# Neighbourhood attention in a two-layer hybrid block: value products of two heads side by side on the column halves of the array

## The chip, the core and the metric

The kernel runs on one core of one Trainium2 chip. The metric is device time in microseconds (us); lower is better. The engines of the core are named as in the profile: PE (TensorE, the matrix multiplier; PEld is its weight load), DVE (VectorE), ACT (ScalarE), POOL (GpSimd), and SP, whose queue issues most transfers. A matmul reads its stationary operand (the weights) and its moving operand from on-chip memory and writes PSUM; DVE and ACT copy PSUM back.

## The reference, cut to what matters

The block has two layers over 512 latent tokens (a grid of 8 rows by 64 columns) and 256 context tokens, with 1024 features. Layer 0 mixes tokens with eight neighbourhood-attention heads of 64 features and four mLSTM heads, layer 1 with latent attention; each layer ends with a gated feed-forward network. All of it is computed to float32 accuracy. The part at issue is the neighbourhood attention:

```python
s_lat = jnp.einsum('bqhd,bkhd->bhqk', q_row, k_band).astype(jnp.float32) * scale + bias
s_ctx = jnp.einsum('bqhd,bkhd->bhqk', q_row, k_c).astype(jnp.float32) * scale
p = jax.nn.softmax(jnp.concatenate([s_lat, s_ctx], axis=-1), axis=-1).astype(v.dtype)
return (jnp.einsum('bhqk,bkhd->bqhd', p[..., :nl], v_band)
        + jnp.einsum('bhqk,bkhd->bqhd', p[..., nl:], v_c))
```

The context tokens have an attention of their own over the 256 context keys (`dense_attention`), with the same heads.

## The kernel before

**How the work is tiled.** The queries of a head are cut into four column strips of the grid, 128 queries each (index `j`). A strip sees 256 latent keys (two key tiles of 128) and the 256 context keys (two more), so its scores are one PSUM tile of 128 queries by 512 keys, named `sp`. Softmax runs along that row: DVE adds the bias and takes the maximum, ACT takes the exponential, POOL divides by the sum; the result is `P[j]`.

**Value products.** For the product with the values, keys must lie on the partitions. For a key tile `ks` the kernel transposes the four `P[j]` on PE into a PSUM tile `ptp`, copies it to `pT` (128 keys by 512 queries), and multiplies: `vtok` (128 keys by 64 features of one head) is the stationary operand, `pT` the moving one. The output `ops` has the 64 features on its partitions: head 0 of a pair on partitions 0 to 63, head 1 on 64 to 127 (`rows`). So each product uses 64 of the array's 128 columns, which the profile shows as the form `128*64` (rows by columns of the array in use). Key tiles 2 and 3 (context) are one product of 512 columns; key tiles 0 and 1 (latent) are four of 128 columns, since each strip has its own values. These operands are plain float32, and the trace has two matmul records for each such instruction. The context tokens go the same way: `scores_c`, the transposes `ptc`, the copy `pTc`, and two products of 256 columns into `opc`.

**Order.** Pairs of heads run one after the other (`p_` 0 to 3). While a pair is in attention, `fill(n)` puts in steps of the projections of the next pair (`qp`, `kp`, `vp`, and the transposes `vtp` that make the next `vtok` from the copies `vt`); while the last pair is in attention, steps of the output projection (`yps`). The scores and projections use another float32 format (one record each). A scheduler places each engine's instructions once, before the run; on the chip each engine goes through its list in that order. In `before` a head is taken alone: `weighted(0)`, then `weighted(1)`, then `weighted_c` for either head.

**Other names.** `whi` and `wlo` are the two parts of a weight unit of 1024 columns, split by ACT and DVE from the loaded `wraw`; `spc`, `mxc`, `lsc` and `Pc` are scores, maximum, sum and weights of the context tokens; `mix` takes the outputs of all heads; `av` and `aw` belong to the modulation of layer 1, which DVE works out during the last pair; `fcw` holds the convolution weights of the feed-forward networks.

Of the kernel before, what the change touches and what calls it, by code (L numbers as in the profile page):

```python
# [9 lines left out]
F32 = mybir.dt.float32  # L10
# [8 lines left out]
TX = 512  # L19
TC = 256  # L20
T = TX + TC
# [45 lines left out]
def hybrid_backbone_kernel(ctx: ExitStack, tc: tile.TileContext, *aps):  # L67
# [14 lines left out]
    def psum_open(**n):  # L82
        """n: tiles per tag; A tiles hold two banks, the others one"""
        if psum:
            psum["st"].close()
        st = ExitStack()
        psum["st"], psum["n"], psum["split"] = st, n, False
        psum["p"] = st.enter_context(tc.tile_pool(name="ps" + "".join(f"{k}{v}" for k, v in n.items()), bufs=1,
                                                  space=bass.MemoryType.PSUM, reuse_waits="tile"))
# [41 lines left out]
    fcw = cload("ffn_conv", [128, 2, 2 * NH, 4])  # L131
# [26 lines left out]
    def table(func, after):  # L158
        """has the activation table loaded ahead of its first use"""
# [23 lines left out]
    def proj(o, w, x, cols, ks=tuple(range(KD)), first=True, last=True):  # L183
        """out[m, cols] = sum over k tiles of W[k, m]^T x[k, cols]; w units hold [k][128]."""
# [60 lines left out]
    def ada(l, part, get, pool, bufs):  # L245
        """modulation part (1024 columns) of layer l; column group j of the array takes 256 of them"""
# [19 lines left out]
    def ada_q(l, part, q, get, pool, bufs):  # L266
        """256 columns of a part; column group j of the array takes a quarter of the k tiles"""
# [16 lines left out]
    def ada_v(l, part, hf, nv, get, pool):  # L284
        """half a part of the modulation on the vector engine: the k tiles are scaled and added up, then the
        tensor engine sums over the partitions"""
# [40 lines left out]
    def mod_scale(l, part, norm, name, nv=2):  # L327
        """norm_g * (1 + scale)"""
# [14 lines left out]
    class Seg:  # L343
        """a run of tokens: width, offset in the padded layout, offset in the packed one, modulation column"""
# [12 lines left out]
    def rstd_bc(pss, n, dim, name):  # L357
        """PSUM [128, n*128]: rstd of every token on all partitions"""
# [16 lines left out]
    def step(n):  # L375
        """n steps of the norm chains in flight, oldest first"""
# [7 lines left out]
    def until(sg):  # L384
        """finish the chain of a run of tokens"""
# [3 lines left out]
    def sums4(ps, w, srcs, first, last):  # L389
        """column sums of four tiles, side by side in the array"""  # L390
# [4 lines left out]
    def sums_bc(ps, sg, name):  # L395
        """rstd on all partitions from the sums of sums4"""
# [7 lines left out]
    class YNorm:  # L404
        """sum of squares over the feature tiles of a branch output, then the gated residual"""
# [27 lines left out]
        def chain(self, x, y, Gt, mod=None, done=None):  # L433
            """x(k) += y(k) * rstd * G, then h hi/lo = split(x(k) * rstd * A + B) with mod = (A, B, h), or done(k);
            a feature tile per step, y as scratch"""
# [38 lines left out]
    # =============================== layer 0 ===============================  # L474
# [4 lines left out]
    with ExitStack() as l0:  # L479
# [38 lines left out]
        def x0_scale(q):  # L518
            """x * rstd * A for a quarter of the feature tiles"""
# [16 lines left out]
        def token_major(which, wus):  # L536
            """W[k, 512] with tokens on the output partitions; a k tile per step"""
# [39 lines left out]
        # gate rows, four feature tiles side by side in the array; the shift comes in with the bias  # L577
# [58 lines left out]
        # tri[:, 0]: k <= m ; tri[:, 1]: k >= m ; tri[:, 2]: row 127 ; tri[:, 3]: row 0  # L636
# [12 lines left out]
        # additive masks: msk[:, 0] allows column <= row, msk[:, 1] allows column >= row  # L649
# [9 lines left out]
        # running maxima of e along the scan, chunks and heads on partitions (the directions 32 apart)  # L659
# [52 lines left out]
        # -M in three exact pieces (rows 0, 32, 64 on), for its sums over the partitions to be rows of it  # L712
# [30 lines left out]
        def na_proj(p_, nq, res):  # L743
            """queries, keys and values of a pair of heads, in steps"""
# [46 lines left out]
        def na_attn(p_, nw, bias_t, fill, qs, kd, kl, vtok):  # L791
# [34 lines left out]
            def weighted(s, P):  # L826
                r0, r1 = rows[s]
                for ks in (2, 3, 0, 1):
# [4 lines left out]
                    pT = nw.tile([128, 512], F32, tag="pT", name="pT", bufs=2)  # L833
                    if ks % 2:
# [3 lines left out]
                    if ks >= 2:  # L838
                        mm(ops_[r0:r1, 0:TX], vtok[:, 7 + ks - 2, r0:r1], pT, ks == 2, False)
                    else:  # L840
                        for j in range(4):
                            vi = VTILE[KSTART[j] + 16 * ks]
                            mm(ops_[r0:r1, j * 128:(j + 1) * 128], vtok[:, vi, r0:r1],
                               pT[:, j * 128:(j + 1) * 128], False, ks == 1 and j == 3)

            def scores_c(s):
# [12 lines left out]
                Pc = nw.tile([128, 512], F32, tag="P", name="Pc", bufs=8)  # L859
# [9 lines left out]
            def weighted_c(s, Pc, opc):  # L869
                r0, r1 = rows[s]  # L870
# [6 lines left out]
                pT = nw.tile([128, 512], F32, tag="pT", name="pTc", bufs=2)  # L877
                V.tensor_copy(out=pT, in_=pt)
                for kt in range(2):
                    mm(opc[r0:r1, 0:TC], vtok[:, 7 + kt, r0:r1], pT[:, kt * 256:(kt + 1) * 256],  # L880
                       kt == 0, kt == 1)
# [7 lines left out]
            weighted(0, P0)  # L889
            c0 = scores_c(0)  # L890
            weighted(1, P1)
            act(mix[:, p_, 0:TX].rearrange("p (r j c) -> p j r c", j=4, r=8),
                ops_.rearrange("p (j r c) -> p j r c", j=4, r=8))
            c1 = scores_c(1)
            opc = ps_x("opc")
            weighted_c(0, c0, opc)
            weighted_c(1, c1, opc)
# [791 lines left out]
```

## Time and profile before

| | |
|---|---|
| device time, 3 runs | 1885.5 to 1888.87 us, median 1886.98 us |
| span of the profiled execution | 1887.4 us, from its first instruction to its last |
| PE busy | 97% of the span |
| DVE, ACT, POOL busy | 62%, 40%, 14% |
| neighbourhood attention | about 285 to 505 us of the span |

The profiled execution's span lies within the runs' range, 0.4 us above their median, and nothing of note lies around it. In the rows, a line of the timeline gives the start, the time until the last of the merged instructions ends, the engine, the line of the program, the operation, output and input names, the form, and the count of records. Matmul durations overlap, since matmuls are pipelined: what an instruction costs PE is read from the distance between starts.

### The profile page before, as it was taken

The numbers are of one execution on the slowest core, as the hardware profiler recorded it, in microseconds if no ns is written. First come the engines' busy times: TensorE is split into PE (matmuls) and PEld (weight loads), VectorE is DVE, ScalarE is ACT, GpSimd is POOL, SyncE is SP. The second block draws the span as 40 slices with busy tenths as digits, with TensorE's granted clock in tenths as the row PEclk, the third lists the DMA queues.
The fourth block names the chain that finished last, engine by engine and source line by source line (L and its number), as shares of the span: only waits on it lengthen the run. The fifth ranks groups of instructions, "written<-read, shape, count | busy, mean of one in ns | idle before, by whom it ended". The sixth has DMA issues, their size and how long they took to land. (4 is left out here: it accounts for less than half of the span.)

```text
span 1887.4 us, 26712 instructions
## 1 busy us (share of the span) xinstructions
PE 1825.2 (97%) x10546; PEld 1492.1 (79%) x10546; DVE 1173.2 (62%) x2230; ACT 748.0 (40%) x1295; POOL 258.8 (14%) x312
## 2 busy tenths in 40 slices
PE   7999999999999999999999999899998999999997
PEld 4777787776678888888888887778887888888885
DVE  3383676345537676767666456888885574556655
ACT  3333454343334432222221334567784444334232
POOL 1000132122222000000000002444451100000000
PEclk8999999999999999999999999999999999999998
DMA  8343431112310333434432210100011213333221
GB/s 300 107 134 112 135 101 48 48 51 78 117 40 28 107 123 112 124 111 145 134 112 78 79 57 24 41 12 13 12 34 56 68 58 99 101 94 118 89 90 45
DMA packets 63196, 162.26 MB, mean 86 GB/s; under 512 B 6256, under 2 KB 19744, under 8 KB 63072
## 3 DMA queue, kind: packets, MB, share of 16 engines
q1 hardware_dynamic: 61616, 156.52, 26.4%
q0 software_dynamic: 1312, 3.91, 0.6%
q8 instruction: 83, 1.36, 0.3%
q14 instruction: 41, 0.34, 0.1%
q10 hardware_dynamic: 144, 0.13, 0.0%
HBM read 158.44 MB, written 2.10 MB: 85 GB/s over the span
## 5 line engine op out<-in xcount | busy, mean ns | idle before, releaser
L147 ACT ACTIVATE whi<-wraw 128x1024 fp32r<-128x1024 f32 x186 | 195.5, 1059 | 466.3 <-PE pu L141 220.0
L150 DVE TENSOR_TENSOR wlo<-wraw,whi 128x1024 fp32r<-128x1024 f32 x183 | 222.9, 1224 | 223.6 <-ACT whi L147 218.0
L141 PE MATMUL pu<-h,whi 128*128 128x258 f32 (+1 forms) x1280 | 318.6, 339 | 0.0
L141 PEld LDWEIGHTS pu<-h,whi 128*128 128x128 f32 x1280 | 219.7, 189 | 28.6 <-issue 0.8
L141 PE MATMUL pd<-hid,whi 128*128 128x512 f32 (+1 forms) x864 | 233.3, 358 | 1.5 <-DVE acc L150 1.5
L141 PE MATMUL pu<-h,wlo 128*128 128x512 f32 (+1 forms) x640 | 216.8, 339 | 0.0
L141 PEld LDWEIGHTS pd<-hid,whi 128*128 128x128 f32 x864 | 152.3, 188 | 28.4 <-DVE acc L150 3.1
L150 POOL TENSOR_TENSOR ry<-rv,mhalf 128x2 f32<-128x2 f32 (+2 forms) x26 | 23.8, 915 | 1013.9 <-DVE rv L153 1011.9
L141 PE MATMUL pd<-hid,wlo 128*128 128x512 f32 (+1 forms) x432 | 153.1, 356 | 0.0
L156 DVE SCALAR_TENSOR_TENSOR u<-pu,c_ffn_conv,u 128x769 f32<-128x769 f32 (+1 forms) x156 | 138.0, 885 | 21.6 <-ACT u L147 19.7
L150 DVE TENSOR_TENSOR acc<-pd,acc 128x512 f32<-128x512 f32 (+1 forms) x192 | 109.2, 586 | 48.6 <-PE pd L141 47.3
L141 PEld LDWEIGHTS pu<-h,wlo 128*128 128x128 f32 x640 | 121.0, 189 | 13.6
L141 PE MATMUL pu<-lb,whi 128*128 128x512 f32 x304 | 119.7, 394 | 0.0
L141 PE MATMUL pu<-hb,whi 128*128 128x512 f32 x304 | 119.0, 391 | 0.0
L141 PE MATMUL pu<-hb,wlo 128*128 128x512 f32 x304 | 118.3, 389 | 0.0
L156 DVE SCALAR_TENSOR_TENSOR av<-aw,s,av 128x512 f32<-128x512 f32 x140 | 102.4, 749 | 20.4 <-DMA aw<-in_ada_w_dram 19.9
L153 POOL TENSOR_SCALAR P<-P,rl 128x768 f32<-128x768 f32 (+1 forms) x96 | 85.6, 893 | 148.3 <-DVE nm L153 60.5
L141 PEld LDWEIGHTS pd<-hid,wlo 128*128 128x128 f32 x432 | 81.2, 189 | 11.7
L147 ACT ACTIVATE u<-pu,c_ffn_conv 128x770 f32<-128x770 f32 (+1 forms) x78 | 68.4, 877 | 39.5 <-PE pu L141 39.4
L141 PE MATMUL sp<-kr,qh 128*128 128x512 f32 (+1 forms) x256 | 72.6, 359 | 4.3 <-DVE kr L150 3.3
L141 PE MATMUL yps<-h,whi 128*128 128x512 f32 (+1 forms) x256 | 69.6, 360 | 0.0
L141 PEld LDWEIGHTS pu<-hb,whi 128*128 128x128 f32 x304 | 57.1, 188 | 13.2
(442 smaller groups left out, 3861.6 us busy)
## 6 DMA issues: line engine op xcount, KB each, us to landing
wraw<-in_ffn_up_dram SPq DMA_DIRECT2D x88, 512.0 KB, 3.6
aw<-in_ada_w_dram SPq DMA_DIRECT2D x112, 256.0 KB, 2.7
wraw<-in_ffn_down_dram SPq DMA_DIRECT2D x44, 512.0 KB, 3.6
aw<-in_ada_w_dram SPq DMA_DIRECT2D x40, 512.0 KB, 4.7
wraw<-in_w_in_dram SPq DMA_DIRECT2D x20, 512.0 KB, 3.6
wraw<-in_w_tok_dram SPq DMA_DIRECT2D x8, 512.0 KB, 4.2
wraw<-in_w_out_dram SPq DMA_DIRECT2D x8, 512.0 KB, 3.5
wraw<-in_w_o_dram SPq DMA_DIRECT2D x8, 512.0 KB, 3.5
```

The costliest lines, as they stand in the source:

```text
L141: PE.matmul(out=o, lhsT=l, rhs=r, start=start, stop=stop)
L147: S.activation(out=o, in_=i, func=func, **kw)
L150: e.tensor_tensor(out=o, in0=x, in1=y, op=op)
L153: e.tensor_scalar(out=o, in0=x, scalar1=s1, scalar2=s2, op0=op0, op1=op1)
L156: V.scalar_tensor_tensor(out=o, in0=x, scalar=s, in1=y, op0=op0, op1=op1)
```

## The change

For each key tile the weights of both heads are transposed (`turned`), and the products follow one key tile later (`products`), the two heads' instructions in turns. ACT makes the copy of head 0 and DVE that of head 1; before, they took turns by key tile. `pT` has four buffers in place of two, and `Pc` two buffers of its own in place of two of `P`'s eight. The context scores of head 0 come before all transposes, those of head 1 after the second key tile; the context transposes and products are arranged in the same manner. To make room, the convolution weights of layer 1 are loaded into a tile of their own at the start of that layer's output projection, by POOL's queue. Comments were removed too.

```diff
-            def weighted(s, P):
-                r0, r1 = rows[s]
-                for ks in (2, 3, 0, 1):
+            def turned(ks, Ps):
+                pts = []
+                for s, P in enumerate(Ps):
                     pt = ps_w("ptp")
                     for j in range(4):
                         tr(pt[:, j * 128:(j + 1) * 128], P[j][:, ks * 128:(ks + 1) * 128])
                     fill(nf[1])
-                    pT = nw.tile([128, 512], F32, tag="pT", name="pT", bufs=2)
-                    if ks % 2:
+                    pT = nw.tile([128, 512], F32, tag="pT", name="pT", bufs=4)
+                    if s:
                         V.tensor_copy(out=pT, in_=pt)
                     else:
                         act(pT, pt)
-                    if ks >= 2:
-                        mm(ops_[r0:r1, 0:TX], vtok[:, 7 + ks - 2, r0:r1], pT, ks == 2, False)
-                    else:
-                        for j in range(4):
...
+                    pts.append(pT)
+                return pts
+            def products(ks, pts):
+                if ks >= 2:
+                    for s, (r0, r1) in enumerate(rows):
+                        mm(ops_[r0:r1, 0:TX], vtok[:, 7 + ks - 2, r0:r1], pts[s], ks == 2, False)
+                    return
+                for j in range(4):
+                    vi = VTILE[KSTART[j] + 16 * ks]
+                    for s, (r0, r1) in enumerate(rows):
+                        mm(ops_[r0:r1, j * 128:(j + 1) * 128], vtok[:, vi, r0:r1],
+                           pts[s][:, j * 128:(j + 1) * 128], False, ks == 1 and j == 3)
...
-                Pc = nw.tile([128, 512], F32, tag="P", name="Pc", bufs=8)
+                Pc = nw.tile([128, 512], F32, tag="Pc", name="Pc", bufs=2)
...
-            weighted(0, P0)
-            c0 = scores_c(0)
-            weighted(1, P1)
+            cs = [scores_c(0)]
+            late = None
+            for ks in (2, 3, 0, 1):
+                pts = turned(ks, (P0, P1))
+                if late:
+                    products(*late)
+                late = (ks, pts)
+                if ks == 3:
+                    cs.append(scores_c(1))
+            ptc = [turned_c(0, cs[0])]
+            products(*late)
             act(mix[:, p_, 0:TX].rearrange("p (r j c) -> p j r c", j=4, r=8),
                 ops_.rearrange("p (j r c) -> p j r c", j=4, r=8))
-            c1 = scores_c(1)
+            ptc.append(turned_c(1, cs[1]))
             opc = ps_x("opc")
-            weighted_c(0, c0, opc)
-            weighted_c(1, c1, opc)
+            for kt in range(2):
+                for s, (r0, r1) in enumerate(rows):
+                    mm(opc[r0:r1, 0:TC], vtok[:, 7 + kt, r0:r1], ptc[s][:, kt * 256:(kt + 1) * 256],
+                       kt == 0, kt == 1)
...
+    fcw.append(accp.tile([128, 2 * NH, 4], F32, name="fcw1"))
+    nc.gpsimd.dma_start(out=fcw[1], in_=a["ffn_conv"][:, 1])
```

On PE, in the first pair, these are the first product of head 0 before the change, with the instructions around it (numbers after a name are buffers; `kp` is a projection, `ptp` a transpose):

```order
L144 MATMUL ptp_2948<-c_ident_70,P_2735 128x128
L141 MATMUL ops_2726<-pT_2945,vtok_2524 64x512
L141 MATMUL kp_2935<-h1_116,whi_2754 128x512
L141 MATMUL kp_2935<-h0_115,wlo_2755 128x512
L141 MATMUL kp_2935<-h0_115,whi_2754 128x512
```

And this is the first key tile of both heads on PE now, followed by that pair's third key tile further down:

```order
L141 MATMUL kp_2937<-h0_115,wlo_2755 128x256
L141 MATMUL ops_2726<-pT_2972,vtok_2524 64x512
L141 MATMUL ops_2726<-pT_2988,vtok_2524 64x512
L141 MATMUL spc_3024<-kd1_2461,qs1_2191 128x256
...
L141 MATMUL ops_2726<-pT_3075,vtok_2524 64x128
L141 MATMUL ops_2726<-pT_3091,vtok_2524 64x128
L141 MATMUL ops_2726<-pT_3075,vtok_2524 64x128
```

What moved: an instruction of head 0 (`pT_2972`, `pT_3075`) now stands right ahead of one of head 1 (`pT_2988`, `pT_3091`).

At the end of the first pair PE's list now reads as follows; before, the fourth key tile's products stood together, and so did each head's two context products:

```order
L144 MATMUL ptc_3135<-c_ident_70,Pc_2952 128x128 x4
L141 MATMUL ops_2726<-pT_3109,vtok_2524 64x128
L144 MATMUL vtp_3141<-c_ident_70,vt_3142 128x128 x4
L144 MATMUL vtp_3141<-c_ident_70,vt_3148 128x128 x3
L141 MATMUL ops_2726<-pT_3125,vtok_2524 64x128
L141 MATMUL ops_2726<-pT_3109,vtok_2524 64x128
L144 MATMUL vtp_3154<-c_ident_70,vt_3155 128x128 x2
L141 MATMUL ops_2726<-pT_3125,vtok_2524 64x128
L141 MATMUL ops_2726<-pT_3109,vtok_2524 64x128
L141 MATMUL ops_2726<-pT_3125,vtok_2524 64x128
L141 MATMUL ops_2726<-pT_3109,vtok_2524 64x128
L141 MATMUL ops_2726<-pT_3125,vtok_2524 64x128
```

What moved: the fourth key tile (`pT_3109` of head 0, `pT_3125` of head 1) is cut into pieces of one, two and five instructions by the next pair's value transposes. The context products behind it stand as one of head 0, two score instructions, and then three.

On ACT, at the same place, the split of the next weight unit stood behind the first two copies of the next pair's values before:

```order
L147 ACTIVATE vt_3152<-vp_3046 128x8x4x16
L147 ACTIVATE vt_3158<-vp_3046 128x8x3x16
L147 ACTIVATE whi_3218<-wraw_3216 128x1024
L147 ACTIVATE vt_3165<-vp_3046 128x256
```

Now it stands ahead of them:

```order
L147 ACTIVATE pT_3109<-ptp_3095 128x512
L147 ACTIVATE whi_3218<-wraw_3216 128x1024
L147 ACTIVATE vt_3142<-vp_3040 128x8x4x16
L147 ACTIVATE vt_3148<-vp_3040 128x8x3x16
L147 ACTIVATE pTc_3160<-ptc_3135 128x512
L147 ACTIVATE vt_3155<-vp_3040 128x256
```

What moved: `whi` went ahead of both `vt` copies, and the context copy `pTc` of head 0, which was DVE's, came in ahead of the third.

## Rows read from the trace of the kernel before

**Rows 1.** The page: PE's share, granted clock by slice, one group of transfers.

```profile
PE 1825.2 (97%) x10546; PEld 1492.1 (79%) x10546; DVE 1173.2 (62%) x2230; ACT 748.0 (40%) x1295; POOL 258.8 (14%) x312
PEclk8999999999999999999999999999999999999998
wraw<-in_ffn_up_dram SPq DMA_DIRECT2D x88, 512.0 KB, 3.6
```

**Rows 2.** Busy time of each engine over the neighbourhood attention; PEclk is granted clock.

```profile
285.00:505.00 220.00, 217.17 (x1072) 152.17 (x1072) 113.79 (x295) 77.42 (x171) 55.53 (x84) 0.97 0.19 58
```

**Rows 3.** Timeline of PE in the first pair: start, time, operation, count.

```profile
310.34 0.60 PE L144 MATMUL ptp<-c_ident,P 128*128 128x128 f32 x4
310.69 0.48 PE L141 MATMUL kp<-h,whi 128*128 128x512 f32 x1
...
326.35 0.62 PE L141 MATMUL vp<-h,whi 128*128 128x512 f32 x2
326.81 0.39 PE L141 MATMUL vp<-h,wlo 128*128 128x512 f32 x1
327.13 1.07 PE L141 MATMUL ops<-pT,vtok 128*64 128x512 f32 x2
328.14 0.66 PE L144 MATMUL ptp<-c_ident,P 128*128 128x128 f32 x4
328.55 0.72 PE L141 MATMUL vp<-h,whi 128*128 128x512 f32 x2
```

**Rows 4.** Timeline of PE in the last pair: products without other work between.

```profile
480.92 2.85 PE L141 MATMUL ops<-pT,vtok 128*64 128x512 f32 x12
483.70 0.66 PE L144 MATMUL ptp<-c_ident,P 128*128 128x128 f32 x4
...
485.92 1.89 PE L141 MATMUL ops<-pT,vtok 128*64 128x128 f32 x10
487.74 1.09 PE L144 MATMUL ptp<-c_ident,P 128*128 128x128 f32 x8
```

**Rows 5.** Timeline of PE: plain float32 instructions on quarters of the array's columns.

```profile
85.45 2.83 PE L581 MATMUL gps<-mix,wg 128*32 128x512 f32 x32
88.06 0.64 PE L141 MATMUL gps<-mod,wg 128*32 128x2 f32 x16
...
112.88 0.41 PE L305 MATMUL adav<-av,ones_v 128*32 128x128 f32 x2
113.21 0.63 PE L141 MATMUL clp<-cm,tri 128*128 128x24 f32 x4
...
114.78 0.43 PE L305 MATMUL adav<-av,ones_v 128*32 128x128 f32 x8
115.13 0.50 PE L141 MATMUL vtk<-whi,h 128*128 128x512 f32 x1
```

**Rows 6.** Timelines of ACT and PE where PE waits, with idle time and releaser.

```profile
451.40 1.06 ACT L147 ACTIVATE whi<-wraw 128x1024 fp32r<-128x1024 f32 x1 [0.31 <-PE vp L141]
452.36 0.96 ACT L147 ACTIVATE vt<-vp 128x512 f32<-128x512 f32 x2
...
452.99 0.98 PE L144 MATMUL vtp<-c_ident,vt 128*128 128x128 f32 x7 [1.08 <-ACT vt L147]
...
499.25 0.44 PE L144 MATMUL ptc<-c_ident,Pc 128*128 128x128 f32 x2 [1.06 <-POOL Pc L153]
```

**Rows 7.** PE's starts before, and sp's and yps's counts in, the stretch at half clock.

```profile
460.73 0.39 PE L141 MATMUL sp<-kd,qs 128*128 128x256 f32 x1
461.04 0.38 PE L141 MATMUL sp<-kl,qs 64*128 64x256 f32 x1
...
464.40:477.90 13.50, 6.30 (x14) 3.76 (x13) 2.77 (x4) 0.00 (x0) 0.51 0.41 153
...
464.40:477.90 13.50, 8.08 (x16) 5.21 (x17) 0.00 (x0) 0.51 0.41 153
```

More of the change, by code (lines that the diff above doesn't have):

```diff
@@ L130, in hybrid_backbone_kernel @@
     mlg = cload("ml_g", [128, MLH])
-    fcw = cload("ffn_conv", [128, 2, 2 * NH, 4])
+    fcw = [cload("ffn_conv", [128, 2 * NH, 4], a["ffn_conv"][:, 0])]
     qng = cload("q_norm_g", [128, 2])
@@ L837, in weighted @@
                         act(pT, pt)
-                    if ks >= 2:
-                        mm(ops_[r0:r1, 0:TX], vtok[:, 7 + ks - 2, r0:r1], pT, ks == 2, False)
-                    else:
-                        for j in range(4):
-                            vi = VTILE[KSTART[j] + 16 * ks]
-                            mm(ops_[r0:r1, j * 128:(j + 1) * 128], vtok[:, vi, r0:r1],
-                               pT[:, j * 128:(j + 1) * 128], False, ks == 1 and j == 3)
+                    pts.append(pT)
[10 more added lines that the diff above has]
+                           pts[s][:, j * 128:(j + 1) * 128], False, ks == 1 and j == 3)
             def scores_c(s):
@@ L867, in scores_c, with turned_c @@
                 return Pc
-            def weighted_c(s, Pc, opc):
-                r0, r1 = rows[s]
+            def turned_c(s, Pc):
                 pt = ps_w("ptc")
@@ L876, in weighted_c @@
                 fill(nf[3])
[L877 to L881, printed above, removed]
+                pT = nw.tile([128, 512], F32, tag="pT", name="pTc", bufs=4)
+                if s:
+                    V.tensor_copy(out=pT, in_=pt)
+                else:
+                    act(pT, pt)
+                return pT
             P0 = scores(0)
@@ L1161, in up_post @@
                     u = fw.tile([128, pw], F32, tag=f"u{g}", name=f"u{g}")[:, c0:c0 + w]
-                    cw = fcw[:, l, g * NH + j, :]
+                    cw = fcw[l][:, g * NH + j, :]
                     act(u, pu, AF.Identity, scale=cw[:, 1:2], bias=cw[:, 3:4])
```

## Prediction

> **What bounds the kernel now.** I read the page first: PE is busy for 97% of the span, and the other engines for much less [rows 1]. So the question is what PE spends on the part that changes, and whether anything else takes over. The busy times over the neighbourhood attention come next: PE 217.17 of 220 us, DVE 113.79, ACT 77.42 and POOL 55.53 [rows 2]. In this stage, too, PE sets the pace, and the other three have room. Since matmul durations overlap, I then read the timeline by distances between starts, at the value products in the first and the last pair [rows 3, 4]. Last I looked for work elsewhere in the trace that already puts different instructions on different column groups [rows 5], for the stage's few idle places [rows 6], and for the stretch in which the clock drops [rows 7].
>
> **What a product costs now.** In the last pair three products stand together: 12 records, from which to the next instruction 2.78 us pass; two others, 10 records, take 1.82 us. One alone takes 1.01 us [rows 3, 4]. So each further product costs (2.78 + 1.82 - 2 x 1.01) / 3 = 0.86 us, and 0.15 us of the single one is the end of a block. A block costs something on either side as well: the projection instruction ahead starts 0.32 us before it, where 0.23 us is usual (two in the 0.46 us from 326.35), so 0.09 us more; the four transposes behind it take 0.41 us until the next start, where 0.35 us is usual, so 0.06 us more [rows 3]; I take 0.08, since what follows differs from block to block. A block of products thus has a fixed cost of about 0.15 + 0.09 + 0.08 = 0.32 us, whatever is in it. I call this a change of form (from 128 by 128 to 128 by 64 of the array and back). A pair has ten products' worth of work: four key tiles for two heads, and the context products, which come to one product's worth of columns for each head.
>
> **What overlap is worth.** No row shows two halves of the array at work together; the nearest show quarters. One `adav` instruction (two records) takes 0.33 us to the next start; four of them on four different column groups (eight records) take 0.35 us. And 32 `gps` records, eight of 512 and eight of 256 columns' instructions, take 2.61 us [rows 5]. By the price above (0.86 us for 512 columns alone) they would take 8 x (0.86 + 0.43) = 10.3 us one after the other, so they ran practically four abreast. These are plain float32 instructions with different moving operands, writing different partitions of the same PSUM tile, as the two heads' products do. The ends of the bound for two halves are full overlap (0.86 us for two products) and none (1.72); I take full overlap, to which the rows are nearest.
>
> The Trainium skill has a rule that speaks against this ("TensorE: Matmul & The Clock Gate", Part 3, "The mechanism"): matmuls start and end strictly in program order. The `gps` instructions stand in the program as 512 and 256 columns on one column group, then the same on the next, so by that rule little of them could overlap; the 2.61 us do not agree with it. What it would make of this change is the second rival.
>
> **The sum.** *First three pairs.* Before: ten blocks of one product, 10 x (0.86 + 0.32) = 11.8 us. After: three blocks that each hold one key tile of both heads, at 0.86 of work; the fourth key tile in three pieces (one, then one on either half, then five with three on one half: 0.215 + 0.215 + 0.645 = 1.08 us at a quarter product each); the context in two pieces (0.43, then three instructions with two on one half, 0.86). That is 2.58 + 1.08 + 1.29 = 4.95 us of work, in eight blocks with 8 x 0.32 = 2.56: 7.5 us. The saving is 4.3 us a pair, 12.9 for three.
>
> *Last pair.* Before: ten products in seven blocks, 8.6 + 2.24 = 10.84 us. After: the first key tile's two products stand apart (0.86 each), three key tiles overlap, the context is as above: 5 x 0.86 + 1.29 = 5.59, again in seven blocks: 7.83. The saving is 3.0.
>
> *Waits.* Two of the idle places change. In the last pair PE waited 1.06 us for `Pc`, whose scores now come two key tiles earlier: gone. At the end of the third pair it waited 1.08 us for `vt`, behind a `whi` of 1.06 us on ACT [rows 6]; that order on ACT now holds in the first two pairs too. From the last `vp` instruction to a first `vt` ACT needs 1.06 us and half of 0.96, with some start 1.7 us. PE has in between the third key tile (0.86 + 0.32), four transposes (0.35) and one product piece (0.215 + 0.32), together 2.1 us: covered, and if it were not, each pair would lose at most the 1.08 us seen. I count the 1.06 as gained, leave the third pair's wait as it is, and set 0.6 against it for new short waits, above all of the context products for the copies that come right ahead of them.
>
> *The rest.* Copies and transposes keep their number; four context copies move from DVE to ACT, which is idle for nearly two thirds of the stage [rows 2]. Without that cover one would cost about half a microsecond, as a `vt` copy does [rows 6]. The second half of `fcw` is one more transfer on POOL, needed only by the feed-forward network behind the output projection, which hides it; if late, it would cost about the 3.6 us in which a larger transfer lands [rows 1], once. More buffers cost nothing. What follows the stage waits on PE or for weights that are loaded while the last pair runs, so I expect it only to begin earlier.
>
> Together 12.9 + 3.0 + 1.06 - 0.6 = 16.4 us. From the profiled span of 1887.4 this leaves 1871.0; that span lies 0.4 us above the median of the runs, so I predict 1870.6 us against 1886.98.
>
> **Rivals.**
> 1. *The halves overlap in part.* If an instruction could start only when the one ahead of it in the program had started its last record, a pair of 512-column products would take three record times (3 x 0.43 = 1.29 us), not two: 0.43 more for two key tiles (one in the last pair), about 0.1 for each of the others and 0.2 for the context. That is 1.3 us a pair, 5 in all: about 1875.5. With waits on top it reaches 1880. This is also what the rule named above would give. Against it: [rows 5].
> 2. *No overlap.* Then only the blocks get fewer, 37 to 31, 6 x 0.32 = 1.9 us: about 1885, no change that can be told. The change would not do what it says. For it there is only that no row shows the form 128 by 64 with both halves in use.
> 3. *The clock.* At 464.4 the granted clock fell to 0.51 for 13.5 us, after a stretch in which PE was busy by the record but alternated between forms in the scores [rows 7]. That stretch holds 14 `sp` and 16 `yps` records; at full clock, 0.31 and 0.23 us apiece [rows 3, 7], they take 8.0 us, so it cost 5.5. The change takes solid work out of each pair's end and leaves the scores, so the first or second pair may now fall to the lower of the two levels (1.2 GHz, not 2.4) as well. One more such stretch: 1876. This is also the rival on the other side: four more (22 us) are needed to be slower by over 0.2%, about 1892.5; three make it even. Against it: the page's clock line stays at 9 in these slices [rows 1], and the projections between the scores of the first three pairs are denser than `yps` in the last.
>
> **How the numbers follow.** Chances: as forecast, 12 to 21 us saved, 0.72; partial overlap 0.11; one or two clock stretches more 0.08; no overlap 0.04; slower by the clock 0.03; more than 21 us saved, if the old clock stretch or the waits go too, 0.02. Faster by over 0.2% (3.8 us, about what a measurement of this kernel can tell from no change) is the sum of the first three and the last, 0.93; no change 0.04; slower 0.03. The likeliest case by itself spans 1866 to 1875. For 8 in 10 I take in most of rival 1 and the single clock stretch: 1865.5 to 1879.
>
> **What would show it.** In the changed profile, two `ops` products of 512 columns (four records) should take about 1.0 us to the next start, not 1.9; PE's busy time on `ops` and `opc` should fall by nearly half; the first three pairs should each be some 4.3 us shorter, the last 3. If four such records take 1.4 us, rival 1 holds; if 1.9, rival 2. A second stretch of lower clock between 290 and 450 us would be rival 3. A wait of PE for `vt` or `pTc` of over a microsecond in each pair would show my cover wrong, and PE idle behind 500 us that the stages behind don't simply begin earlier.

## The result

| | before | after |
|---|---|---|
| device time, median (lowest to highest) | 1887.34 us (1885.5 to 1888.87, 4 runs) | 1870.51 us (1868.35 to 1873.8, 4 runs) |
| ratio of the times, 95% interval | | 0.9915 [0.9901, 0.9929] |
| span of the profiled execution | 1887.4 us | 1868.9 us |

16.8 us, or 0.85%, are gained; the prediction was 1870.6 us, 16.4 us less than before. The page of the changed kernel answers to [rows 1]: PE has 16.3 us less to do in as many instructions, and the line of the granted clock (tenths of full speed) is again at 9 in nearly every slice.

```profile
PE 1808.9 (97%) x10546; PEld 1483.8 (79%) x10546; DVE 1171.6 (63%) x2226; ACT 751.7 (40%) x1299; POOL 262.9 (14%) x313
...
PEclk8999999998999999999999999899999999999998
```

The busy times of the engines by stretch, of the changed kernel, answer to [rows 2]. The first line is the same stretch of the span, the others run from one mark to the next: the start of the last `vp` instruction ahead of each of the four pairs, and the first statistics (`pssy`) of the stage behind (columns: us, then busy time of PE, weight loads, DVE, ACT, POOL, then the granted clock, the DMA share and GB/s).

```profile
285.00:505.00 220.00, 220.00 (x1155) 159.72 (x1154) 117.65 (x297) 89.31 (x188) 66.04 (x89) 0.96 0.24 75
277.95:334.08 56.13, 56.04 (x332) 43.38 (x330) 35.17 (x115) 26.42 (x58) 17.61 (x24) 1.00 0.23 68
334.08:384.38 50.30, 50.30 (x283) 37.34 (x282) 22.75 (x54) 20.56 (x43) 11.32 (x16) 1.00 0.16 48
384.38:434.70 50.32, 50.32 (x283) 37.30 (x282) 29.03 (x62) 20.27 (x43) 18.65 (x26) 1.00 0.16 48
434.70:520.97 86.27, 86.27 (x404) 61.06 (x403) 36.10 (x77) 29.51 (x59) 24.39 (x28) 0.90 0.31 104
```

The same four stretches between the same marks of the kernel before:

```profile
277.31:340.52 63.21, 63.11 (x364) 47.05 (x362) 35.20 (x114) 25.94 (x56) 16.15 (x22) 1.00 0.19 62
340.52:395.86 55.34, 55.26 (x284) 39.38 (x282) 23.16 (x55) 19.55 (x43) 9.89 (x16) 1.00 0.14 43
395.86:451.20 55.34, 55.27 (x284) 39.37 (x282) 28.64 (x63) 19.26 (x42) 15.75 (x26) 1.00 0.14 43
451.20:539.50 88.30, 85.63 (x373) 61.17 (x372) 37.17 (x79) 28.40 (x60) 26.67 (x30) 0.92 0.32 102
```

Read them side by side: the two middle pairs are 5.0 us shorter each, the first 7.1, the last part 2.0; together 19.2 us. (After the change 32 records of each of the first three pairs, the third and fourth key tile with 1.03 and 1.53 us, stand behind the next mark; before, they stood ahead of it. This makes the first difference larger by about 2.6 us and the last one smaller by as much.) In the last stretch before, PE was idle for 2.7 of 88.30 us; after, for nothing. The stage begins 0.64 us later, since an early stretch of low clock is longer (in the window from 144 to 154 us the granted clock is 0.66, before 0.83).

PE's timeline in the first pair of the changed kernel, at the value products, answers to [rows 3]:

```profile
320.46 1.08 PE L141 MATMUL ops<-pT,vtok 128*64 128x512 f32 x4
321.47 0.39 PE L141 MATMUL spc<-kd,qs 128*128 128x256 f32 x1
...
334.28 1.09 PE L141 MATMUL ops<-pT,vtok 128*64 128x128 f32 x16
335.31 0.66 PE L144 MATMUL ptc<-c_ident,Pc 128*128 128x128 f32 x4
335.89 0.43 PE L141 MATMUL ops<-pT,vtok 128*64 128x128 f32 x2
336.25 0.98 PE L144 MATMUL vtp<-c_ident,vt 128*128 128x128 f32 x7
337.17 0.44 PE L141 MATMUL ops<-pT,vtok 128*64 128x128 f32 x4
337.54 0.44 PE L144 MATMUL vtp<-c_ident,vt 128*128 128x128 f32 x2
337.90 0.87 PE L141 MATMUL ops<-pT,vtok 128*64 128x128 f32 x10
338.70 0.66 PE L144 MATMUL ptc<-c_ident,Pc 128*128 128x128 f32 x4
```

Two 512-column products, four records, take 1.01 us to the next start, which is what one took [rows 3]; the sixteen records of a latent key tile take 1.03. The fourth key tile stands in the three pieces that the order had shown, and they take 0.36, 0.37 and 0.80 us: 1.53 together, half a microsecond more than in one block. No `vtp` waits for `vt` here.

Last, the place where the half clock starts in the last pair, as [rows 7] before:

```profile
439.74 0.36 PE L141 MATMUL sp<-kd,qs 128*128 128x256 f32 x1
...
445.38 0.38 PE L141 MATMUL sp<-kl,qs 64*128 64x256 f32 x1
445.70 0.38 PE L141 MATMUL sp<-kd,qs 128*128 128x256 f32 x1
446.01 0.51 PE L141 MATMUL sp<-kl,qs 64*128 64x256 f32 x1
446.45 0.58 PE L141 MATMUL sp<-kd,qs 128*128 128x256 f32 x1
446.96 0.58 PE L141 MATMUL sp<-kl,qs 64*128 64x256 f32 x1
```

```profile
446.00:463.10 17.10, 17.10 (x37) 10.48 (x37) 8.49 (x32) 6.38 (x18) 6.41 (x9) 0.50 0.31 120
```

From 446 us the distance between score starts grows from 0.31 to 0.51 us, and the clock is at its lower level (1.2 GHz, granted clock 0.50: the half clock) for 17.1 us. Before, it was 13.7 us, both read from the trace's records of the granted clock ([rows 7] show 13.5 of it). Ahead of it PE had run score instructions of two forms in turns, with a few context products and no projection, from 439.7 us on.

Where a pair's 5.03 us come from is seen by adding up, for the second pair, the distance of each PE start to the next, by the tile that the instruction writes (two of the experiments below stand beside it):

| us in the second pair | before | after | one half (first experiment) | products last |
|---|---|---|---|---|
| `ops`, 40 records | 8.08 | 4.58 | 7.65 | 4.07 |
| `opc`, 8 records | 2.02 | 1.58 | 1.59 | 1.01 |
| `ptp`, 32 | 3.38 | 2.89 | 2.89 | 2.89 |
| projections `qp`, `kp`, `vp`, 144 | 27.89 | 27.34 | 27.54 | 27.54 |
| `sp`, `spc`, 40 | 11.77 | 11.63 | 11.64 | 11.66 |
| `ptc`, `vtp`, 17 | 2.20 | 2.28 | 2.13 | 2.43 |
| sum | 55.34 | 50.31 | 53.45 | 49.61 |

### The profile page after: what moved, and what is told of

Same layout as the page of the kernel before. It is cut to its first block, busy times and chain, and to the rows that moved or that the text cites. A ratio compares the mean times of both kernels' runs of the same rounds, so it can differ in the third digit from the quotient of the medians.

```text
span 1868.9 us, 26713 instructions
## 1 busy us (share of the span) xinstructions
PE 1808.9 (97%) x10546; PEld 1483.8 (79%) x10546; DVE 1171.6 (63%) x2226; ACT 751.7 (40%) x1299; POOL 262.9 (14%) x313
## 4 chain that ended last, share of the span: by engine, by line
PE 87%; DVE 5%; POOL 2%; issue 2%; ACT 2%; DMA 2%; DVEq 0%; POOLq 0%; ACTq 0%
PE pu L141 28%; PE pd L141 13%; PE yps L141 5%; PE sp L141 5%; PE qkp L141 3%; PE puf L141 3%; PE qp L141 3%; PE pdl L141 3%; PE vtk L141 3%; PE kp L141 2%; PE pt L144 2%; PE vp L141 2%; PE ot L141 2%; PE ops L141 1%; PE ysum L392 1%
## 5 line engine op out<-in xcount | busy, mean ns | idle before, releaser
L141 PEld LDWEIGHTS pu<-h,wlo 128*128 128x128 f32 x640 | 120.9, 189 | 13.7
L156 DVE SCALAR_TENSOR_TENSOR u<-pu,c_ffn_conv,u 128x769 f32<-128x769 f32 x80 | 81.2, 1014 | 10.1 <-ACT u L147 9.4
L141 PEld LDWEIGHTS pu<-hb,wlo 128*128 128x128 f32 x304 | 57.1, 188 | 13.1
L150 DVE TENSOR_TENSOR pTl<-pt,pTh 128x512 fp32r<-128x512 f32 x96 | 64.6, 682 | 4.4 <-ACT pTh L147 3.7
```

The costliest lines, as they stand in the source:

```text
L141: PE.matmul(out=o, lhsT=l, rhs=r, start=start, stop=stop)
L150: e.tensor_tensor(out=o, in0=x, in1=y, op=op)
L156: V.scalar_tensor_tensor(out=o, in0=x, scalar=s, in1=y, op0=op0, op1=op1)
```

## Experiments

The theory was: the two heads' products run at the same time on the two column halves, and this, with a few changes of form less, is the gain. The rivals: the new order alone does it (fewer blocks, fewer waits, later products); or the halves overlap only as far as the order in turns lets them. All changes are made to the changed kernel unless it is said otherwise, and times are medians over a kernel's runs; the kernel before was run beside each (medians 1886.50 to 1887.62 us).

**Both heads on one half.**

```diff
-mm(ops_[r0:r1, 0:TX], vtok[:, 7 + ks - 2, r0:r1], pts[s], ks == 2, False)
+w0, w1 = rows[ks % 2]
+mm(ops_[w0:w1, 0:TX], vtok[:, 7 + ks - 2, r0:r1], pts[s], s == 0, False)
```

(and likewise for the other key tiles, with `rows[kt]` for the context)

> Both heads' products of a key tile go to the same column half (key tiles 2 and 0, and the first context tile, into partitions 0 to 63; 3 and 1 and the second into 64 to 127), so the attention's outputs are changed; the instructions, their shapes and nearly their order stay. If the gain is from two halves at work together, it goes: per pair 3 x 0.86 + 0.64 + 0.43 = 3.65 us more in the first three, 3.0 in the last, 14.0 in all: about 1884.5, and two 512-column products take 1.87 us to the next start instead of 1.01. If it is from the new order (fewer blocks, fewer waits, later products), nothing is lost: 1870.5.

1880.20 us (1874.14 to 1882.94, 6 runs), ratio to before 0.9958 [0.9943, 0.9972]: 9.7 us of the 16.8 are lost, where 14.0 were expected; these runs scatter more than the others, and the profiled execution is the longest of the six. Its timeline, and the windows of its first two pairs:

```profile
320.82 1.93 PE L141 MATMUL ops<-pT,vtok 128*64 128x512 f32 x4
322.69 0.39 PE L141 MATMUL spc<-kd,qs 128*128 128x256 f32 x1
```

```profile
276.81:336.14 59.33, 59.24 (x331) 44.95 (x330) 35.30 (x115) 26.35 (x58) 17.63 (x24) 0.97 0.20 65
336.14:389.59 53.45, 53.45 (x283) 39.35 (x282) 22.93 (x54) 20.47 (x43) 11.35 (x16) 1.00 0.14 45
```

Two products take 1.87 us to the next start, to the hundredth as expected, and the second pair is 3.14 us longer. 3.65 was expected; the context products lost nothing (1.59 us in the table, 1.58 after), because the second context tile was sent to the other half and so ran beside the first. Without that 0.43 the expectation is 3.22. The whole stage is 14.7 us longer (257.7 against 243.0 between the marks), with a short stretch of lower clock in the first pair among it, which the changed kernel has not (granted clock 0.97 there). So the overlap is shown, and so is that it isn't everything: with no overlap in `ops` a pair is still 1.89 us shorter than before. 0.43 of that lie in `opc`, whose products still overlap here; about 1.5 of a pair's 5.03 us are left for the order, with the reserve that the fourth key tile stands in two pieces in this run and in three in the changed kernel.

**How far the order in turns is needed.** Four products of head 0 ahead of four of head 1:

```diff
-for j in range(4):
-    vi = VTILE[KSTART[j] + 16 * ks]
-    for s, (r0, r1) in enumerate(rows):
+for s, (r0, r1) in enumerate(rows):
+    for j in range(4):
+        vi = VTILE[KSTART[j] + 16 * ks]
```

> For the two key tiles with four products a head, the four of head 0 now stand ahead of the four of head 1, not in turns. If a half draws its instructions past those that wait for the other half, as far as four ahead, nothing changes: 1870.5, and sixteen records take 1.0 us. If an instruction starts only when the one ahead of it in the program has started its last record, seven of the eight stand one behind the other: 7 x 0.215 = 1.5 us instead of 0.86, 0.65 more in two key tiles of four pairs, 5.2 us in all: about 1875.7.

And in twos (the line stands in place of both loops):

```diff
+for s, j in ((0, 0), (0, 1), (1, 0), (1, 1), (0, 2), (0, 3), (1, 2), (1, 3)):
```

> In the two key tiles with four products a head, two products of head 0 stand ahead of two of head 1, and so on in twos. If each half has one place for an instruction that waits while another runs, the second of head 0 takes that place, head 1's first starts at once, and nothing is lost: sixteen records in 1.0 us, 1870.5. If a half has no such place, and it takes the next instruction of the program only when that can start, the sixteen take (8 + 2) / 8 of that or more, 1.25 to 1.5 us, and the kernel 1872.5 to 1875.

By fours 1871.63 us (0.9920 [0.9908, 0.9932]), by twos 1870.38 (0.9906 [0.9892, 0.9920]): neither can be told from the changed kernel by its time, but the timeline tells them apart, where a latent key tile stands whole (by fours, then by twos).

```profile
334.04 1.58 PE L141 MATMUL ops<-pT,vtok 128*64 128x128 f32 x16
335.56 0.65 PE L144 MATMUL ptc<-c_ident,Pc 128*128 128x128 f32 x4
```

```profile
334.72 1.15 PE L141 MATMUL ops<-pT,vtok 128*64 128x128 f32 x16
335.80 0.66 PE L144 MATMUL ptc<-c_ident,Pc 128*128 128x128 f32 x4
```

In turns it was 1.03 us; by twos it is 1.08, by fours 1.52. So of four instructions of head 0 in a row, two run alone (2 x 0.215 = 0.43, of the 0.49 more), and of two in a row none does. The first half microsecond of these tiles says the same: eight records of `ops` have started in turns (the first line), four by fours (the second; the count stands behind the first busy time).

```profile
334.24:334.74 0.50, 0.46 (x8) 0.46 (x10) 0.00 (x0) 1.00 0.00 0
```

```profile
334.00:334.50 0.50, 0.46 (x4) 0.46 (x5) 0.00 (x0) 1.00 0.00 0
```

The trace also tells the heads apart, since head 1's first product alone waits for DVE's copy: by fours it starts at 334.54 us, together with head 0's third product and 0.21 us ahead of head 0's fourth, which stands ahead of it in the program. It is as if each half had one instruction running and a place for one that waits, and the program were handed out in order until a place is missing; both runs fit this, and no run tests it further. Neither expectation for four was right: not "nothing lost", nor 0.65 per key tile. Strict turns are not required.

**Copies by key tile, and products without delay.**

```diff
-                    if s:
+                    if ks % 2:
                         V.tensor_copy(out=pT, in_=pt)
```

> The copies of the transposes are shared out as in the kernel before: both heads' copies of a key tile on one engine, all context copies on DVE. If the copies lie under PE's other work, nothing changes: 1870.5, at most 2 us more from the last pair and the ends of the pairs. If the change's gain rested on the two copies side by side, the second copy comes about 0.5 us later for each of 5 tiles in 4 pairs, and up to 10 us are lost: 1880.

```diff
-                pts = turned(ks, (P0, P1))
-                if late:
-                    products(*late)
-                late = (ks, pts)
+                products(ks, turned(ks, (P0, P1)))
```

> Products are written right behind the transposes of their key tile, not behind those of the next. In the first three pairs there is projection work enough to stand between, so no change there; in the last pair, with 14 steps to fill, each key tile may wait about 1 us for its copies, 2 to 4 us together: 1872 to 1874. If the late products are what carries the gain, four waits of about 1.2 us in each pair come back: about 1889.

1870.19 us (0.9909 [0.9894, 0.9923]) and 1868.84 us (0.9900 [0.9886, 0.9913]): both as the changed kernel. The second pair takes 50.70 and 50.12 us. That the heads share the two copying engines, and that the products come a key tile late, is worth nothing that can be measured here; the 2 to 4 us that the second was expected to lose did not show. So neither the copies nor the delay carries the gain, and the first experiment showed that the order as a whole is the smaller part of it.

**Fewer blocks.** The fourth key tile's products uncut, once by priority, once by being written behind both context transposes:

```diff
+            with tc.high_priority(offset=100):
+                products(*late)
```

> The fourth key tile's products get a higher priority, so that they stand as one block right behind the third's (32 records together) and no longer in three pieces among the transposes of the next pair's values. By the fixed cost of a block (0.32 us) and the 0.22 us of product pieces without a partner, each pair is 3 x 0.32 + 0.22 = 1.2 us shorter, 4.7 in four pairs, unless PE then waits for the copies that are just being made: with 0.5 us of wait a pair it is 2.7 us. So 1866 to 1868; if blocks cost nothing by themselves, 1870.

```diff
-            products(*late)
             act(mix[:, p_, 0:TX].rearrange("p (r j c) -> p j r c", j=4, r=8),
                 ops_.rearrange("p (j r c) -> p j r c", j=4, r=8))
-            ptc.append(turned_c(1, cs[1]))
```

(and both lines stand ahead of `act`, the `ptc` line first)

> The fourth key tile's products are written behind the transposes of both heads' context weights, and so stand in one block, and the context's in one or two. No wait for copies is then possible, and the saving is the same: two blocks and a piece less in each pair, 2 x 0.32 + 0.22 = 0.9 us, up to 3.5 in all: 1867. If blocks cost nothing by themselves, 1869.6 (the pieces alone). The result is evicted later, which only the last pair could feel (about 1 us).

1868.75 us (0.9903 [0.9888, 0.9918]) and 1864.27 us (0.9886 [0.9870, 0.9903]). By priority the second pair shrank from 50.31 to 49.94 us only: `ops` fell by 0.66, but the context transposes were now the ones to be cut up (+0.33), and `opc` went in among the next projections (`qp` +0.17). Written last, the pair is 49.61 us, the third 49.37. Its timeline in the first pair:

```profile
339.06 1.09 PE L141 MATMUL ops<-pT,vtok 128*64 128x128 f32 x16
340.08 0.39 PE L141 MATMUL sp<-kd,qs 128*128 128x256 f32 x1
...
341.77 1.08 PE L141 MATMUL opc<-pTc,vtok 128*64 128x256 f32 x8
342.79 0.50 PE L141 MATMUL qp<-h,whi 128*128 128x512 f32 x1
```

The pieces of 0.36, 0.37 and 0.80 us have become one of 1.02, and the context one of 1.02 instead of 0.58 and 1.00. The second pair is 0.70 us shorter and the third 0.95, near the 0.9 that a block's price gave. Most of the rest of the 6 us lies in the last part:

```profile
434.38:516.40 82.02, 81.76 (x405) 59.20 (x404) 36.20 (x77) 29.12 (x59) 23.49 (x28) 0.94 0.34 109
```

It is 82.02 us instead of 86.27, and the half clock in it lasts 10.2 us instead of 17.1. That the order of the products shortens the half clock is not shown by this: the run without delay has 10.2 us too.

**The half clock.** Steps of the output projection behind the scores of the last pair (the four numbers are the steps behind a score tile, a key tile's transposes, the context's scores and its transposes):

```diff
-NF3 = (0, 1, 2, 3)
+NF3 = (1, 1, 0, 0)
```

> In the last pair one step of the output projection (three matmuls of 512 columns) is put behind each score tile, and none behind the context's. If the long stretch of half clock (17 us in the changed kernel, which cost about 8.5) comes from the scores that stand there alone, it goes or gets short: 1862 to 1866. If it has to do with something else, it stays, and the steps are then missing behind the transposes: 1870 to 1873.

With (2, 0, 0, 0), that is two steps behind each score tile and none elsewhere:

> As the run with one step behind each score tile, but with two, so that nothing is left for the key tiles. The half clock in the scores should be gone if it comes from scores that stand alone (8.5 us less), but each of four key tiles may then wait up to 1 us for its copies, and a stretch of half clock may come there: 1864 to 1870.

And (1, 1, 0, 0) in the kernel before:

> The kernel before, with one step of the output projection behind each score tile of its last pair. If the half clock there comes from scores that stand alone whatever form the products have, the same edit takes it away here: 13.7 us of it cost about 6, so about 1881. If it hangs together with how the value products are written, nothing or little changes: 1885 to 1888.

1862.41 us (0.9875 [0.9860, 0.9890]), 1866.42 us (0.9888 [0.9874, 0.9903]) and 1883.13 us (0.9977 [0.9968, 0.9986]); the last is 4.5 us under the kernel before, where about 6 were expected. Windows of the first at the place of the half clock, and its last part:

```profile
446.00:463.10 17.10, 16.06 (x67) 10.61 (x68) 11.85 (x38) 7.23 (x20) 7.78 (x10) 1.00 0.43 153
...
434.69:513.67 78.98, 77.94 (x405) 56.75 (x404) 36.22 (x77) 29.50 (x59) 25.68 (x28) 1.00 0.36 114
```

The clock stays at its upper level and the last part is 7.3 us shorter (86.27 to 78.98), although a wait of 1.0 us for `P` has come in. The same edit in the kernel before gives the last part at granted clock 1.00, and 82.89 us instead of 88.30 (0.7 of that are shorter waits):

```profile
454.73:537.62 82.89, 80.96 (x373) 57.13 (x371) 36.68 (x79) 28.64 (x60) 25.60 (x30) 1.00 0.33 108
```

So the half clock goes with the scores that stand alone, whatever form the value products have: filled up, it is gone in all four profiled executions that have such an edit, and it is there in all ten that have not. Its length is another matter: it is 10.2, 13.7 or 17.1 us in these ten. With two steps a score it is gone as well, but the key tiles then stand in pieces (the last part is 79.33 us), and this execution has a short stretch of half clock in its first pair (57.65 us instead of 56.13), as the first experiment, the two with other copies and delay, products last and by twos have too.

**The last pair by itself.** The first three pairs as after, the last as before:

```diff
+            if p_ == 3:
+                weighted(0, P0)
+                c0 = scores_c(0)
+                weighted(1, P1)
...
+                return
```

(`weighted` and `weighted_c` are those of the kernel before, but with four buffers of `pT`, and `Pc` keeps the two of its own.)

> The first three pairs run as in the changed kernel, the last as in the kernel before. By the prediction's terms the last pair is worth 3.0 us of products and 1.06 us of the wait for Pc: the stage is 4.1 us longer than in the changed kernel, about 1874.5. If the longer stretch of half clock (17.1 us against 13.7) belongs to the new last pair, 1.7 us come back: about 1873. If the last pair gains nothing, 1870.5 or less.

1870.93 us (0.9910 [0.9897, 0.9924]), not to be told from the changed kernel. Its last part:

```profile
433.39:521.06 87.67, 87.36 (x405) 62.56 (x404) 37.15 (x78) 28.82 (x58) 24.80 (x28) 0.92 0.31 102
```

It is 1.4 us longer than after (86.27). The half clock lasts 13.7 us here and 17.1 after. The 3.4 us between them cost 1.3 to 1.6, by estimate: in the half clock a score starts every 0.51 us instead of 0.31, a `yps` every 0.43 instead of 0.23. So the new form is worth about 3 us in the last pair, and the clock takes about half of that back. The distances between starts agree: `ops` and `opc` take 13.70 us in this part here and 10.80 after, 2.9 less. PE's view of waits is empty here between 430 and 520 us: the waits for `Pc`, `pTc` and `vt` are gone although the last pair has its old order.

**Products last and the fill together.**

> The fourth key tile's products written last, and one step of the output projection behind each score tile of the last pair, both at once. If the two gains lie in different places they add: 2.7 us of fewer blocks and about 7.3 us for the half clock gone, from 1870.5 to about 1860.5. If fewer blocks only helped by shortening the half clock, nothing is added to the 1862.4 of the fill alone.

1860.11 us (1859.70 to 1860.77, 4 runs), ratio to before 0.9852 [0.9840, 0.9865], and so the fastest version: 27.5 us under the kernel before that was run beside it. The gains add, as far as they lie in different places: products last gave 6.2 us by itself and 2.3 on top of the fill, near the 2.7 expected of its blocks, since the fill alone has already done away with the half clock.

```profile
386.72:436.09 49.37, 49.37 (x284) 37.03 (x282) 28.95 (x62) 20.20 (x43) 18.66 (x26) 1.00 0.16 49
436.09:513.06 76.97, 76.56 (x405) 56.25 (x404) 35.66 (x77) 29.56 (x59) 23.69 (x28) 1.00 0.36 117
```

## Why the prediction was right

*PE bounds the stage.* It held, more strictly than before: 220.00 of 220 us. Behind the stage nothing changed (1347.9 us from the last mark to the end in both), so the gain is all in it.

*Full overlap.* Right in kind and in size. The sum had 3.65 us less product work in each of the first three pairs (8.6 to 4.95). `ops` and `opc` together fell by 3.94 (10.10 to 6.16), of which two block ends of 0.15 are 0.30, so the work fell by 3.64. The distances thus fell by 39%, and PE's busy time on the two tiles by 36% (42.5 to 27.3 us, from 300 to 510 us), not by the "nearly half" among the signs: the blocks' ends and the pieces without a partner stay.

*Starts in program order.* What such a rule would make of the change is the first rival; the prediction calls it "the second" in one place. In twos a key tile took 0.05 us more than in turns, and by fours head 1's first product started ahead of head 0's fourth. The Trainium skill ("TensorE: Matmul & The Clock Gate", Part 3, "The mechanism") states that matmuls start and end strictly in program order. These two runs do not agree with it: by that order a key tile in twos would have taken 0.2 us more, by estimate.

*A block's fixed cost.* The step that was mis-sized. Two blocks fewer were to save 0.64 us a pair; 0.30 of it are the ends, and 0.34 was left for the neighbours. The neighbours gave 1.1 (5.03 less 3.94): transposes 0.49, projections 0.55, scores 0.14, less 0.08 for `ptc` and `vtp`. The price was taken as one for each block; the second pair of the kernel before shows that it depends on the neighbour:

```profile
366.11 0.60 PE L144 MATMUL ptp<-c_ident,P 128*128 128x128 f32 x4
366.73 1.07 PE L141 MATMUL ops<-pT,vtok 128*64 128x512 f32 x2
...
369.69 0.40 PE L141 MATMUL kp<-h,wlo 128*128 128x512 f32 x1
370.02 1.07 PE L141 MATMUL ops<-pT,vtok 128*64 128x512 f32 x2
371.03 0.65 PE L144 MATMUL ptp<-c_ident,P 128*128 128x128 f32 x4
371.44 0.71 PE L141 MATMUL kp<-h,whi 128*128 128x512 f32 x2
```

A projection right ahead of a block takes 0.33 us to the next start instead of 0.23, four transposes right ahead 0.61 instead of 0.35, and four right behind 0.41; the first and the last are the prices that the prediction read, the second is not in it. A score ahead pays nothing (0.31 as always). Before, eight blocks of this pair had a projection right ahead, one had `ptp` ahead and five had `ptp` behind; now it is three, none and one. That is 5 x 0.09 + 0.26 + 4 x 0.06, or 0.95 of the 1.1. The pieces at the pair's seam stand among `ptc`, `vtp` and scores instead, which together take 13.91 us, 0.06 less than before. So a pair gave 5.0 us, not 4.3.

*The last pair.* 3.0 us of products were right (2.9 measured). The 1.06 us of the wait for `Pc` were gained, but the earlier context scores are not needed for it: the wait is gone with the old order too. The trace of before shows what held `Pc` (DVE, then ACT):

```profile
493.49 0.16 DVE L153 TENSOR_SCALAR mxc<-mxc 128x2 f32<-128x2 f32 x1
...
494.93 0.60 ACT L147 ACTIVATE mix<-ops 128x512 f32<-128x512 f32 x1 [3.34 <-PE ops L141]
495.42 0.47 ACT L147 ACTIVATE Pc<-spc,mxc 128x256 f32<-128x256 f32 x1
```

The maximum `mxc` was ready at 493.65 us, but on ACT `Pc` stood behind `mix`, which waited for the last product. With the old order behind three new pairs, `mix` was done 1.9 us ahead of `mxc`. Whether the buffers of its own for `Pc` changed that, or something upstream, was not tried.

*Waits.* 0.6 us were set aside for new ones; there are none. The third pair's 1.08 us for `vt`, which the sum left in place, is gone too, as is one of 0.5 us for `pTc` that the prediction does not name. The cover of 2.1 us between `vp` and `vt` held in all pairs.

*The clock.* The third rival looked for more stretches at the lower level; in the profiled execution the old one is longer by 3.4 us instead, at a price of 1.3 to 1.6. These are single executions: the one by fours, with the same scores, has 13.7 us. The mean granted clock of the runs points the same way, 0.981 to 0.984 in the four after, 0.984 to 0.986 in the four with the last pair as before. The rival was not empty either: of the eleven variants of the changed kernel, six have a short stretch of half clock in the first pair of their profiled execution, worth about 1.5 us. Products last has it, and the same first pair with the fill has not, so it varies from one execution to the next.

*The base.* Here two errors cancelled. The text took the span as the time ("nothing of note lies around it"), but in every run that lists both, the time is 1.9 to 2.2 us above the span (1870.99 and 1868.9 after; 1886.78 and 1884.8 before). So the profiled execution of before took about 1889.4 us, by estimate, more than any of the four runs in the result, and the forecast of 1871.0 was one of the span. The span in fact came out at 1868.9: 18.5 us less, not 16.4. Medians differ by 16.8. The median hit within 0.1 us is therefore partly luck; the saving in the span was short by 2.1. Missing were 0.7 in each of three pairs, the 0.6 set aside, the 1.08 for `vt` and the 0.5 for `pTc`, together 4.3; against them stand the clock in the last pair (1.3 to 1.6) and the later start of the stage (0.6).

## What to carry to other kernels

Products that leave half of the array's columns unused cost the same here singly as in pairs (1.01 us), so look for a partner on the other half and put the two close together in the program; strict alternation is not needed, but four in a row on one half lose (1.52 us instead of 1.03). Count the changes of form and look at what stands on both sides of each: writing a cut block's work a little later gave almost as much here per pair as one key tile's overlap. And read a stage's timeline for stretches at half clock first: one line that spread projection steps over scores that stood alone gave 8 us, half as much as the whole change.

## What the runs showed of the hardware

- Two column halves with plain float32 operands ran side by side at no loss: 4 records in 1.01 us, as 2 records before; 16 in 1.03.
- Starts did not keep the program's order across the halves: by fours, head 1's first product started 0.21 us ahead of head 0's fourth. The times (by twos 1.08 us, by fours 1.52) fit a half that has room for one waiting instruction while another runs; more was not tested.
- A change of form was paid by the neighbour too, and by its kind: ahead of a block a projection took 0.09 us more, four `ptp` transposes 0.26, a score nothing.
- The clock fell to its lower level while PE ran scores of two forms in turns, with a few products of half the columns among them, although PE's records show no gap (0.50 for 17.1 us, from 446 us on); with a projection step of three matmuls behind each score tile it stayed at 1.00.
